# Eighteen of twenty-two block products of a gated MLP through Strassen's seven half products

## The chip, the core and the metric

The kernel runs on one core of a Trainium2 chip. The metric is the device time of one execution in microseconds; three runs of the kernel before took 979.35 to 979.56 us, with a median of 979.55.

## What is computed

One layer of a bidirectional encoder on 512 tokens of 1,024 features, in float32: a mixing part (short gated convolution and three groups of dilated window attention), a norm, and then the part that matters here, a gated MLP with a width-3 convolution over tokens and a last norm:

```
up = h @ w_up + b_up                       # 1024 -> 2 * 2816
a, gte = up[..., :D_FF], up[..., D_FF:]
f = gelu(dwconv3(a, ffn_conv_w) + ffn_conv_b) * gte
ffn = f @ w_down + b_down                  # 2816 -> 1024
h = layer_norm(ALPHA * h + ffn, ln2_g, ln2_b)
```

## The kernel before, in words

A float32 product runs as three matmuls on float32r parts: each operand is split into a high part (ScalarE, a cast by copy) and a low part (VectorE, the difference), and `mm3` (lines 363 to 366) issues high times high, high times low and low times high into one accumulator.

All weights lie in DRAM in the order of use, as chunks of up to 2,048 columns on 128 partitions (`chunk_plan`, line 65). `chunk(name, key)` (line 313) splits chunk i and i + 1 and issues the load of i + 2 from SyncE's queue; raw pieces of 1,024 columns have 3 buffers, high parts of 2,048 columns 3, low parts of 1,024 columns 5. The scheduler of the language orders each engine's instructions by program order and by when their inputs and buffers are ready, so splits can run further ahead than `chunk` asks.

The MLP has 22 blocks of 128 hidden features (lines 886 to 913). A hidden block takes two products of 24 matmuls on 512 tokens (`unit`, line 368); ScalarE adds the bias, GpSimd shifts rows for the convolution (`pad_shift`, line 669), ScalarE and VectorE convolve, ScalarE applies gelu, VectorE multiplies with the gate (line 907), and the result is split into a tile `f` of high and low part (lines 909, 910). From block 3 to 6 VectorE also scales one token group of the residual (`residual`, line 875).

The product with w_down goes token by token: the four tiles `hb` hold 128 tokens by 1,024 outputs. It comes in two parts, after block 10 and after block 21, each over the eleven blocks of its part and the two halves of 512 outputs. In the first part, and for the first half of the second, four accumulators run beside each other (lines 916 to 923) and VectorE adds each to `hb`. For the last half (lines 925 to 944) each token group takes its 33 matmuls in turn, and VectorE adds, takes statistics (`bn_stats`), finishes mean and deviation (`ln_finish`, line 333) and scales with two `scalar_tensor_tensor` a half; SyncE stores the result. The statistics of the first half are taken beside earlier work (line 931). The last group's half is cut into two times 256 columns, so that less work stands behind the last matmul.

The tiles of weights, activations and sums share one pool of 28 buffers of 1,024 columns (`blk`), the smaller ones another of 13 of 512 (`f32t`). Results of matmuls go through 8 accumulator banks in turn (`ps_any`).

Of the kernel before, what the change touches and what calls it, by code (L numbers as in the profile page):

```python
# [11 lines left out]
P = 128  # L12
# [5 lines left out]
FFH = NFF // 2  # L18
# [46 lines left out]
def chunk_plan():  # L65
# [13 lines left out]
    for part in range(2):  # L79
        for j in range(part * FFH, (part + 1) * FFH):  # L80
            out.append(("up", j, 2048))
        for half in range(2):
            for c, n in ((0, 4), (4, 4), (8, 3)):
                out.append(("dn", (part, half, c, n), n * 512))
    return out


def lay_out_weights(w):
# [10 lines left out]
    for name, key, cols in chunk_plan():  # L99
# [11 lines left out]
        elif name == "gate":  # L111
            c = [block(w_in, (BLK_GA + key) * P, P), block(w_in, (BLK_GB + key) * P, P)]
        elif name == "wo":
            half, kh = key
            c = [block(w_o[kh * 512 : (kh + 1) * 512], half * 512, 512)]
        elif name == "up":
            c = [block(w_up, key * P, P), block(w_up, DFF + key * P, P)]
        else:
            part, half, c0, n = key
            k0 = (part * FFH + c0) * P  # L120
            c = [block(w_down[k0 : k0 + n * P], half * 512, 512)]
# [53 lines left out]
def build(tc, x, wst, colt, dist, rows, vrow, out):  # L175
# [3 lines left out]
    with ExitStack() as ctx:  # L179
# [86 lines left out]
        offs = np.cumsum([0] + [P * c[2] for c in plan])  # L266
        splits = {}

        def load(i):
# [615 lines left out]
        g2 = b2 = None  # L885
        for part in range(2):
            ff = []
            for j in range(part * FFH, (part + 1) * FFH):
                w = chunk("up", j)
                if j < 2:  # L890
                    o = early[2 * j]
                    unit(o, w, 0, h1T, 256, 512)
                else:
                    o = ps_any()
                    unit(o, w, 0, h1T)
                u = small.tile([P, 768], F32, tag="upad", name=f"fp{j}", bufs=2)
                nc.scalar.activation(u[:, 128:640], o, AF.Identity, bias=col(C_BUP + j))  # L897
                pad_shift(u)
                a = conv3(u, C_FW + j, NFF)
                nc.scalar.activation(a, a, AF.Gelu, bias=col(C_FB + j))  # L900
                if j < 2:
                    o = early[2 * j + 1]
                    unit(o, w, 1024, h1T, 256, 512)
                else:
                    o = ps_any()
                    unit(o, w, 1024, h1T)
                nc.vector.scalar_tensor_tensor(a, o, col(C_BUP + NFF + j), a, op0=ALU.add, op1=ALU.mult)
                t = blk(F32R, (2, 512), f"f{j}")
                nc.scalar.activation(t[:, 0], a, AF.Copy)
                nc.vector.tensor_tensor(t[:, 1], a, f(t[:, 0]), op=ALU.subtract)  # L910
                ff.append(t)
                if 3 <= j < 7:
                    residual(j - 3)
            for half in range(2):
                ch = ((0, 4), (4, 4), (8, 3))
                if part == 0 or half == 0:
                    os_ = [ps_any() for _ in range(4)]
                    for c0, n in ch:
                        w = chunk("dn", (part, half, c0, n))
                        for r in range(4):  # L920
                            tok_mm(os_[r], ff, w, range(c0, c0 + n), r, c0, c0 == 0, c0 == 8)
                    for r in range(4):
                        add_to(hb[r], half, os_[r])
                else:
                    g2, b2 = row(6), row(7)
                    ws = [chunk("dn", (part, half, c0, n)) for c0, n in ch]
# [41 lines left out]
```

## Time and profile before

| | us |
|---|---|
| median of three runs | 979.55 |
| the profiled execution | 979.43 |
| its span | 977.6 |
| TensorE busy | 964.9 |
| VectorE busy | 552.9 |
| ScalarE busy | 395.9 |
| GpSimd busy | 55.8 |

The span runs from the first to the last event of the trace; the profiled execution has 1.83 us more around it. PE is TensorE's matmuls, PEld its weight loads, DVE VectorE, ACT ScalarE, POOL GpSimd, SP SyncE. Matmuls are pipelined, so the starts of two neighbours give the time of one better than the duration shown. Waits are put down to the instruction whose semaphore came last.

### The profile page before, as it was taken

How to read it: one execution, taken by the hardware profiler on the slowest of the kernel's cores; microseconds unless marked ns; L12 is line 12 of the kernel's file. 1: busy time of each engine (PE TensorE's matmuls, PEld its weight loads, DVE VectorE, ACT ScalarE, POOL GpSimd, SP SyncE). 2: the span in 40 equal slices, each digit the busy share in tenths (PEclk: the TensorE clock that was granted, in tenths of full speed). 3: DMA queues.
4: the chain of work that ended last, by engine and by line, in shares of the span. 5: the costliest groups of instructions: out<-in, count | busy, mean ns of one | idle time of the engine just before them, and what ended most of it. 6: DMA issues, size and time to landing. Idle time of an engine off the chain costs nothing.

```text
span 977.6 us, 11991 instructions
## 1 busy us (share of the span) xinstructions
PE 964.9 (99%) x4713; PEld 813.9 (83%) x4713; DVE 552.9 (57%) x886; ACT 395.9 (40%) x671; POOL 55.8 (6%) x163
## 2 busy tenths in 40 slices
PE   8999999999999999999999999999999999999996
PEld 7988888887888888888888888988888888888885
DVE  7856755968676444422445667659452255454266
ACT  4644465656543423223433323544441134444220
POOL 1000000000010001001000000011000001000000
PEclk9999999999999999999999999999999999999999
DMA  7313312221222123235324221352323243222412
GB/s 277 108 45 129 108 65 66 87 87 45 87 66 86 66 86 97 98 105 196 115 100 128 88 90 44 127 172 92 103 78 95 88 128 99 96 88 95 129 40 80
DMA packets 28217, 97.29 MB, mean 100 GB/s; under 512 B 3456, under 2 KB 3968, under 8 KB 28160
## 3 DMA queue, kind: packets, MB, share of 16 engines
q1 hardware_dynamic: 25776, 89.60, 28.0%
q0 software_dynamic: 2384, 6.92, 2.3%
q8 instruction: 37, 0.61, 0.3%
q14 instruction: 20, 0.16, 0.0%
HBM read 94.36 MB, written 2.15 MB: 99 GB/s over the span
## 4 chain that ended last, share of the span: by engine, by line
PE 96%; DVE 2%; DMA 1%; issue 0%; ACT 0%; DVEq 0%; POOL 0%; POOLq 0%
PE ps_acc L364 16%; PE ps_acc L366 16%; PE ps_acc L365 16%; PE ps_s L366 5%; PE ps_s L365 5%; PE ps_s L364 5%; PE ps_u L366 5%; PE ps_u L365 5%; PE ps_u L364 5%; PE ps_pt L365 4%; PE ps_pt L366 4%; PE ps_pt L364 4%; PE ps_pt L594 1%; PE ps_u L417 1%; PE ps_acc L417 1%
## 5 line engine op out<-in xcount | busy, mean ns | idle before, releaser
L307 DVE TENSOR_TENSOR lo<-raw,hi 128x1024 fp32r<-128x1024 f32 (+1 forms) x166 | 198.4, 1200 | 237.4 <-ACT hi L295 97.0
L295 ACT ACTIVATE hi<-raw 128x1024 fp32r<-128x1024 f32 x162 | 164.3, 1044 | 238.9 <-PE ps_acc L365 70.3
L364 PE MATMUL ps_acc<-hT,hi 128*128 128x512 f32 x416 | 164.2, 395 | 0.1
L366 PE MATMUL ps_acc<-hT,lo 128*128 128x512 f32 x416 | 162.3, 390 | 0.0
L365 PE MATMUL ps_acc<-hT,hi 128*128 128x512 f32 x416 | 162.0, 390 | 0.0
L366 PEld LDWEIGHTS ps_acc<-hT,lo 128*128 128x128 f32 x416 | 78.1, 188 | 16.7
L364 PEld LDWEIGHTS ps_acc<-hT,hi 128*128 128x128 f32 x416 | 78.2, 188 | 15.7 <-PE ps_acc L366 0.5
L365 PEld LDWEIGHTS ps_acc<-hT,hi 128*128 128x128 f32 x416 | 78.2, 188 | 15.5
L575 ACT ACTIVATE S<-S,nm 128x128 f32<-128x128 f32 (+2 forms) x96 | 40.1, 419 | 35.3 <-DVE nm L573 28.5
L365 PE MATMUL ps_acc<-h1T,hi 128*128 128x512 f32 (+1 forms) x96 | 36.0, 375 | 0.0
L364 PE MATMUL ps_acc<-h1T,hi 128*128 128x512 f32 (+1 forms) x96 | 35.8, 373 | 0.0
L364 PE MATMUL ps_pt<-h1T,hi 128*128 128x512 f32 (+1 forms) x96 | 35.6, 371 | 0.0
L365 PE MATMUL ps_pt<-h1T,hi 128*128 128x512 f32 (+1 forms) x96 | 35.6, 371 | 0.0
L366 PE MATMUL ps_pt<-h1T,lo 128*128 128x512 f32 (+1 forms) x96 | 35.6, 371 | 0.0
L364 PE MATMUL ps_u<-h1T,hi 128*128 128x512 f32 (+1 forms) x96 | 35.6, 371 | 0.0
L365 PE MATMUL ps_u<-h1T,hi 128*128 128x512 f32 (+1 forms) x96 | 35.6, 371 | 0.0
L366 PE MATMUL ps_u<-h1T,lo 128*128 128x512 f32 (+1 forms) x96 | 35.6, 371 | 0.0
L365 PE MATMUL ps_s<-h1T,hi 128*128 128x512 f32 (+1 forms) x96 | 35.6, 371 | 0.0
L364 PE MATMUL ps_s<-h1T,hi 128*128 128x512 f32 (+1 forms) x96 | 35.6, 371 | 0.0
L366 PE MATMUL ps_s<-h1T,lo 128*128 128x512 f32 (+1 forms) x96 | 35.6, 371 | 0.0
L366 PE MATMUL ps_acc<-h1T,lo 128*128 128x512 f32 (+1 forms) x96 | 35.6, 371 | 0.0
L673 POOL COPY fp<-fp 128x127 f32<-128x127 f32 x22 | 14.0, 636 | 317.9 <-ACT fp L897 317.9
(396 smaller groups left out, 2038.8 us busy)
## 6 DMA issues: line engine op xcount, KB each, us to landing
raw<-wst SPq DMA_DIRECT2D x160, 512.0 KB, 3.7
x<-x SPq DMA_DIRECT2D x4, 512.0 KB, 7.1
hb<-x POOLq DMA_DIRECT2D x4, 512.0 KB, 6.4
out<-hb SPq DMA_DIRECT2D x7, 256.0 KB, 2.1
ln_g<-rows POOLq DMA_DIRECT2D x3, 512.0 KB, 5.8
ln_b<-rows POOLq DMA_DIRECT2D x3, 512.0 KB, 7.0
raw<-wst SPq DMA_DIRECT2D x4, 256.0 KB, 2.6
vbias<-vrow POOLq DMA_DIRECT2D x1, 512.0 KB, 8.4
```

The source lines that it names most:

```text
L295: nc.scalar.activation(hi[:, part], Pieces(raws[i])[:, part], AF.Copy)
L307: ins = nc.vector.tensor_tensor(lo[:, part], Pieces(raws[i])[:, part], f(hi[:, part]), op=ALU.subtract)
L364: nc.tensor.matmul(o, ah, bh, start=start, stop=False)
L365: nc.tensor.matmul(o, ah, bl, start=False, stop=False)
L366: nc.tensor.matmul(o, al, bh, start=False, stop=stop)
L417: ins = nc.tensor.matmul(first[n][:, t], wk, hk, start=k == 0 and m == 0, stop=k == KT - 1 and m == 2)
L575: nc.scalar.activation(v, v, AF.Exp, bias=nm[:, j : j + 1], scale=0.125, accum_out=dn[:, j : j + 1])
L594: nc.tensor.transpose(pt[:, j * P : (j + 1) * P], self.pe[:, j * P : (j + 1) * P], ident)
L673: nc.gpsimd.tensor_copy(u[:, 1:128], u[:, 512:639])
```

## The change

Blocks 0 to 17 go in three parts of six blocks, that is three pairs of an even and an odd block. In a part the product is seen as one of 2 x 2 quarters: tokens 0 to 255 and 256 to 511, even and odd blocks, outputs 0 to 511 and 512 to 1,023. Strassen's scheme in Winograd's form makes it with seven products of half size (`STAGES`: Y, X1, W1, X2, V1, W2, V2), each 256 tokens by three blocks by 512 outputs.

The sums of activations (`pair_sums`) are made on VectorE once a pair is there, and split into high and low parts in place of the single blocks. The sums of weights U, T2, T3 and T4 (T2 with a fourth term) are made without an engine: a quarter is loaded plainly from SyncE's queue, and further quarters are added to it by transfers issued on GpSimd's queue that accumulate into the tile (`weight_sums`); signs are put on the activations. The steps are issued after hidden blocks 1 to 4 of a part, the fourth term after the first product. A sum has the columns of three blocks, 1,536, in pieces of 1,024 and 512, and is then split like a chunk; quarters used alone come as chunks.

The seven products of a part are issued after the first hidden block of the next one (`down`). Four of them go to accumulators in SBUF, kept over the three parts (ScalarE copies in the first part, VectorE adds in the others), three straight to `hb`; after the third part VectorE combines them with 16 additions of 512 columns. The last four blocks, 18 to 21, go token by token: for each of the four groups both halves of the outputs are made, added, and normalised; for the first group the matmuls of block 21 come last.

```
@@ -15,7 +15,9 @@
 KT = D // P
 NPAIR = 4
 NFF = 22
-FFH = NFF // 2
+
+NST = 6
+PARTS = 3
...
-    for part in range(2):
-        for j in range(part * FFH, (part + 1) * FFH):
-            out.append(("up", j, 2048))
-        for half in range(2):
-            for c, n in ((0, 4), (4, 4), (8, 3)):
-                out.append(("dn", (part, half, c, n), n * 512))
+    for j in range(NFF):
+        out.append(("up", j, 2048))
+        if j % NST == 0 and j > 0:
+            out += [("sd", (j // NST - 1, s[0]), 1536) for s in STAGES]
+    out += [("dn", half, 2048) for half in range(2)]
     return out
+STAGES = (
+    ("Y", None, "T2"),
+    ("X1", (0, 0), "R"),
+    ("W1", (0, 1), "U"),
+    ("X2", (1, 0), "R"),
+    ("V1", None, "T3"),
+    ("W2", (1, 1), "R"),
+    ("V2", None, "T4"),
+)
+QUARTER = {s[1]: s[0] for s in STAGES if s[1]}
...
+        def quarter(part, x, y):
+            i = where[("sd", (part, QUARTER[x, y]))]
+            return wst[int(offs[i]) : int(offs[i + 1])].rearrange("(p c) -> p c", p=P)
 
...
-        g2 = b2 = None
-        for part in range(2):
-            ff = []
-            for j in range(part * FFH, (part + 1) * FFH):
-                w = chunk("up", j)
...
-            for half in range(2):
-                ch = ((0, 4), (4, 4), (8, 3))
-                if part == 0 or half == 0:
-                    os_ = [ps_any() for _ in range(4)]
-                    for c0, n in ch:
-                        w = chunk("dn", (part, half, c0, n))
-                        for r in range(4):
-                            tok_mm(os_[r], ff, w, range(c0, c0 + n), r, c0, c0 == 0, c0 == 8)
-                    for r in range(4):
-                        add_to(hb[r], half, os_[r])
-                else:
-                    g2, b2 = row(6), row(7)
-                    ws = [chunk("dn", (part, half, c0, n)) for c0, n in ch]
-                    for r in range(4):
...
-                        for i, (a, b) in enumerate(zip(cuts, cuts[1:])):
-                            o = ps_any()[:, : b - a]
-                            for (c0, n), w in zip(ch, ws):
-                                tok_mm(o, ff, w, range(c0, c0 + n), r, c0, c0 == 0, c0 == 8, a - 512, b - 512)
-                            nc.vector.tensor_tensor(z[:, a:b], z[:, a:b], o, op=ALU.add)
-                            nc.vector.bn_stats(out=st[:, 1 + i, :], in_=z[:, a:b])
...
+        def hidden(j):
...
+        def high_low(t, a):
+            nc.scalar.activation(t[:, 0], a, AF.Copy)
+            nc.vector.tensor_tensor(t[:, 1], a, f(t[:, 0]), op=ALU.subtract)
+            return t
+        def pair_sums(i, a0, a1):
+            lo, hi = slice(0, 256), slice(256, 512)
+            k0 = tmp.tile([P, 512], F32R, tag="f32", name=f"k0{i}").rearrange("p (a b) -> p a b", a=2)
+            high_low(k0, a0[:, lo])
+            k1 = high_low(blk(F32R, (2, 512), f"k1{i}"), a1)
+            s13, s24 = f32t("s13"), f32t("s24")
+            nc.vector.tensor_tensor(s13[:, lo], a0[:, hi], a1[:, hi], op=ALU.subtract)
+            nc.vector.tensor_tensor(s13[:, hi], a0[:, lo], a0[:, hi], op=ALU.subtract)
+            nc.vector.tensor_tensor(s24[:, lo], s13[:, lo], a0[:, lo], op=ALU.subtract)
+            nc.vector.tensor_tensor(s24[:, hi], s24[:, lo], a1[:, lo], op=ALU.add)
+            s13 = high_low(blk(F32R, (2, 512), f"s13{i}"), s13)
+            s24 = high_low(blk(F32R, (2, 512), f"s24{i}"), s24)
+            return {"X1": (k0, 0), "X2": (k1, 0), "V2": (k1, 256), "W1": (s13, 0), "V1": (s13, 256), "Y": (s24, 0), "W2": (s24, 256)}
+        sums_of = {}
+        def weight_sums(part, step):
+            R = {q: quarter(part, *q) for q in QUARTER}
+            if step == 0:
+                main = {n: blk(F32, (1024,), f"w{n}") for n in ("U", "T2", "T3")}
+                tails = [blk(F32, (1024,), "wtail") for _ in range(2)]
+                tail = {"U": tails[0][:, :512], "T3": tails[0][:, 512:], "T2": tails[1][:, :512]}
+                for n in main:
+                    sums_of[n] = [main[n], tail[n]]
+                for n, st in (("U", "W1"), ("T2", "Y"), ("T2", "V2"), ("T3", "V1")):
+                    raws[where["sd", (part, st)]] = sums_of[n]
+                todo = [("T2", (0, 0)), ("U", (0, 0)), ("T3", (1, 1))]
+            else:
+                todo = {1: [("T2", (0, 1))], 2: [("U", (0, 1)), ("T3", (0, 1))], 3: [("T2", (1, 1))], 4: [("T2", (1, 0))]}[step]
+            for n, q in todo:
+                for t, src in zip(sums_of[n], (R[q][:, :1024], R[q][:, 1024:])):
+                    if step == 0:
+                        nc.sync.dma_start(out=t, in_=src)
+                    else:
+                        nc.gpsimd.dma_start(out=t, in_=src, accum_op=ALU.add)
+        acc = {}
+        def accumulators():
+            for n, st in enumerate(("X1", "V1")):
+                t = blk(F32, (2, 512), "acc" + st)
+                acc[st] = [t[:, s] for s in range(2)]
+            for st in ("Y", "W1"):
+                acc[st] = [f32t("acc" + st) for _ in range(2)]
+        def down(part, pairs):
+            if part == 0:
+                accumulators()
+            outs = {
+                "X2": [hb[s][:, :512] for s in range(2)],
+                "W2": [hb[s][:, 512:] for s in range(2)],
+                "V2": [hb[2 + s][:, :512] for s in range(2)],
+            }
+            for n, (st, _, _) in enumerate(STAGES):
+                w = chunk("sd", (part, st))
+                for s in range(2):
                     o = ps_any()
+                    for i, pr in enumerate(pairs):
+                        t, c0 = pr[st]
+                        a = slice(c0 + s * P, c0 + (s + 1) * P)
+                        b = slice(i * 512, (i + 1) * 512)
+                        mm3(o, t[:, 0, a], t[:, 1, a], w[0][:, b], w[1][:, b], i == 0, i == len(pairs) - 1)
+                    if st in acc and part == 0:
+                        nc.scalar.activation(acc[st][s], o, AF.Copy)
+                    else:
+                        d = (acc.get(st) or outs[st])[s]
+                        nc.vector.tensor_tensor(d, d, o, op=ALU.add)
+                if n == 0:
+                    weight_sums(part, 4)
+            if part == PARTS - 1:
+                for s in range(2):
+                    x1, y, w1, v1 = (acc[st][s] for st in ("X1", "Y", "W1", "V1"))
+                    (h00, h01), (h10, h11) = ((hb[r][:, :512], hb[r][:, 512:]) for r in (s, 2 + s))
+                    for d, t, op in (
+                        (h00, x1, ALU.add),
+                        (y, x1, ALU.add),
+                        (w1, y, ALU.subtract),
+                        (h01, w1, ALU.add),
+                        (h10, y, ALU.add),
+                        (h10, v1, ALU.add),
+                        (h11, w1, ALU.add),
+                        (h11, v1, ALU.subtract),
+                    ):
+                        nc.vector.tensor_tensor(d, d, t, op=op)
+        pairs, even, ff = [], None, {}
+        for j in range(NFF):
+            a = hidden(j)
+            if j >= PARTS * NST:
+                ff[j] = high_low(blk(F32R, (2, 512), f"f{j}"), a)
+            elif j % 2 == 0:
+                even = a
+            else:
+                pairs.append(pair_sums(j // 2 % (NST // 2), even, a))
+            part, q = divmod(j, NST)
+            if part < PARTS and 1 <= q <= 4:
+                weight_sums(part, q - 1)
+            if 3 <= j < 7:
+                residual(j - 3)
+            if q == 0 and j > 0:
+                down(part - 1, pairs)
+                pairs = []
+        g2, b2 = row(6), row(7)
+        ws = [chunk("dn", half) for half in range(2)]
+        k0 = PARTS * NST
+        for r in range(4):
+            z = hb[r]
+            cuts = (0, 512, 1024) if r < 3 else (0, 512, 768, 1024)
+            parts = list(zip(cuts, cuts[1:]))
+            st = small.tile([P, 3, 6], F32, tag="bnst2", name=f"l2{r}st", bufs=2)
+            o = [ps_any()[:, : b - a] for a, b in parts]
+            def part_sum(i, ks):
+                a, b = parts[i]
+                half = a // 512
+                tok_mm(o[i], ff, ws[half], ks, r, k0, ks[0] == k0, ks[-1] == NFF - 1, a % 512, a % 512 + b - a)
+            if r == 0:
+                for ks in (range(k0, NFF - 1), range(NFF - 1, NFF)):
+                    for i in range(2):
+                        part_sum(i, ks)
+            for i, (a, b) in enumerate(parts):
+                if r > 0:
+                    part_sum(i, range(k0, NFF))
+                nc.vector.tensor_tensor(z[:, a:b], z[:, a:b], o[i], op=ALU.add)
+                nc.vector.bn_stats(out=st[:, i, :], in_=z[:, a:b])
...
```

## Rows read from the trace of the kernel before

**Rows 1.** The page, part 1: busy time by engine.
```profile
span 977.6 us, 11991 instructions
...
PE 964.9 (99%) x4713; PEld 813.9 (83%) x4713; DVE 552.9 (57%) x886; ACT 395.9 (40%) x671; POOL 55.8 (6%) x163
```

**Rows 2.** The page, part 4: the chain that ended last, by engine.
```profile
PE 96%; DVE 2%; DMA 1%; issue 0%; ACT 0%; DVEq 0%; POOL 0%; POOLq 0%
```

**Rows 3.** Busy us of each engine by stretch: PE, PEld, DVE, ACT, POOL; clock, DMA share, GB/s.
```profile
730.00:790.00 60.00, 60.00 (x267) 49.69 (x266) 19.39 (x22) 11.67 (x14) 0.00 (x0) 1.00 0.30 92
790.00:909.00 119.00, 119.00 (x527) 98.57 (x526) 58.34 (x65) 50.41 (x66) 11.70 (x42) 1.00 0.32 102
```

**Rows 4.** PE in order of time, w_down product: start us, us, matmul.
```profile
734.83 0.39 PE L364 MATMUL ps_acc<-hi,f 128*128 128x512 f32 x1
...
745.71 0.39 PE L364 MATMUL ps_acc<-hi,f 128*128 128x512 f32 x1
...
961.26 0.28 PE L364 MATMUL ps_u<-hi,f 128*128 128x256 f32 x1
...
969.06 0.28 PE L366 MATMUL ps_acc<-hi,f 128*128 128x256 f32 x1
```

**Rows 5.** DVE in order of time, last norms: start us, us, operation.
```profile
953.99 0.69 DVE L936 TENSOR_TENSOR hb<-hb,ps_s 128x512 f32<-128x512 f32 x1 [1.43 <-PE ps_s L366]
...
957.20 0.69 DVE L931 BATCH_NORM_STATS2 l23st<-hb 128x6 f32<-128x512 f32 x1
...
958.36 1.41 DVE L943 SCALAR_TENSOR_TENSOR hb<-hb,l21mv,ln_b 128x512 f32<-128x512 f32 x2
...
961.47 0.69 DVE L936 TENSOR_TENSOR hb<-hb,ps_pt 128x512 f32<-128x512 f32 x1 [1.69 <-PE ps_pt L366]
962.19 0.69 DVE L937 BATCH_NORM_STATS2 l22st<-hb 128x6 f32<-128x512 f32 x1
...
966.71 0.41 DVE L936 TENSOR_TENSOR hb<-hb,ps_u 128x256 f32<-128x256 f32 x1
...
969.38 0.42 DVE L936 TENSOR_TENSOR hb<-hb,ps_acc 128x256 f32<-128x256 f32 x1 [1.79 <-PE ps_acc L366]
969.83 0.43 DVE L937 BATCH_NORM_STATS2 l23st<-hb 128x6 f32<-128x256 f32 x1
...
972.79 1.54 DVE L943 SCALAR_TENSOR_TENSOR hb<-hb,l23mv,ln_b 128x512 f32<-128x512 f32 x3
```

**Rows 6.** DVE groups from 600 us on: busy us, mean ns of one.
```profile
L307 DVE TENSOR_TENSOR lo<-raw,hi 128x1024 fp32r<-128x1024 f32 x63 | 77.0, 1224 | 75.8 <-PE ps_pt L366 22.5 <-PE ps_acc L366 19.3 <-PE ps_s L365 15.1
L910 DVE TENSOR_TENSOR f<-cv,f 128x512 fp32r<-128x512 f32 x22 | 15.2, 691 | 4.6 <-ACT f L909 4.6
L361 DVE TENSOR_TENSOR h1T<-lnT,h1T 128x256 fp32r<-128x256 f32 x16 | 6.3, 422 | 0.1
L307 DVE TENSOR_TENSOR lo<-raw,hi 128x512 fp32r<-128x512 f32 x4 | 2.8, 691 | 20.2 <-PE ps_s L365 13.6 <-PE ps_u L365 6.6
L836 DVE TENSOR_TENSOR hb<-hb,ps_u 128x512 f32<-128x512 f32 x4 | 2.7, 686 | 2.3 <-PE ps_u L366 2.3
```

**Rows 7.** ACT groups from 600 us on: busy us, mean ns of one.
```profile
L295 ACT ACTIVATE hi<-raw 128x1024 fp32r<-128x1024 f32 x62 | 62.8, 1054 | 93.1 <-PE ps_s L366 48.3 <-PE ps_u L366 24.1 <-PE ps_s L365 9.1
L897 ACT ACTIVATE fp<-ps_acc,cols 128x512 f32<-128x512 f32 x11 | 7.6, 690 | 30.0 <-PE ps_acc L366 30.0
```

**Rows 8.** Waits from 634 to 968 us: us in total, times, longest us.
```profile
ACT hi L295 <- PE ps_s L366: 48.3, 6, 9.2
...
SPq L277 <- DVE lo L307: 280.6, 57, 11.0
```

**Rows 9.** The page, part 6: DMA issues, KB each, median us to landing.
```profile
raw<-wst SPq DMA_DIRECT2D x160, 512.0 KB, 3.7
...
hb<-x POOLq DMA_DIRECT2D x4, 512.0 KB, 6.4
...
vbias<-vrow POOLq DMA_DIRECT2D x1, 512.0 KB, 8.4
```

More of the change, by code (lines that the diff above doesn't have):

```diff
@@ L117, in lay_out_weights @@
             c = [block(w_up, key * P, P), block(w_up, DFF + key * P, P)]
-        else:
-            part, half, c0, n = key
-            k0 = (part * FFH + c0) * P
-            c = [block(w_down[k0 : k0 + n * P], half * 512, 512)]
+        elif name == "sd":
+            q = dict((s[0], s[1]) for s in STAGES)[key[1]]
+            if q is None:
+                continue
+            k0 = key[0] * NST + q[0]
+            c = [block(w_down[k * P : (k + 1) * P], q[1] * 512, 512) for k in range(k0, k0 + NST, 2)]
+        else:
+            c = [block(w_down[PARTS * NST * P :], key * 512, 512)]
         c = np.concatenate(c, axis=1)
@@ L265, in build @@
         plan = chunk_plan()
-        offs = np.cumsum([0] + [P * c[2] for c in plan])
+        offs = np.cumsum([0] + [P * laid_out(c) for c in plan])
         splits = {}
@@ new lines, in hidden @@
+        def hidden(j):
+            w = chunk("up", j)
+            if j < 2:
+                o = early[2 * j]
+                unit(o, w, 0, h1T, 256, 512)
+            else:
+                o = ps_any()
+                unit(o, w, 0, h1T)
+            u = small.tile([P, 768], F32, tag="upad", name=f"fp{j}", bufs=2)
+            nc.scalar.activation(u[:, 128:640], o, AF.Identity, bias=col(C_BUP + j))
+            pad_shift(u)
+            a = conv3(u, C_FW + j, NFF)
+            nc.scalar.activation(a, a, AF.Gelu, bias=col(C_FB + j))
+            if j < 2:
+                o = early[2 * j + 1]
+                unit(o, w, 1024, h1T, 256, 512)
+            else:
+                o = ps_any()
+                unit(o, w, 1024, h1T)
+            nc.vector.scalar_tensor_tensor(a, o, col(C_BUP + NFF + j), a, op0=ALU.add, op1=ALU.mult)
+            return a
@@ new lines, in build @@
+        pairs, even, ff = [], None, {}
[5 more added lines that the diff above has]
+                even = a
+            else:
+                pairs.append(pair_sums(j // 2 % (NST // 2), even, a))
[7 more added lines that the diff above has]
+                pairs = []
@@ new lines, in build @@
+        g2, b2 = row(6), row(7)
[20 more added lines that the diff above has]
+                nc.vector.bn_stats(out=st[:, i, :], in_=z[:, a:b])
+            ((mean, rstd),) = ln_finish([st[:, : len(parts)]], f"l2{r}")
+            for a, b in parts:
+                s = slice(a, b)
+                nc.vector.scalar_tensor_tensor(z[:, s], z[:, s], mean, g2[:, s], op0=ALU.subtract, op1=ALU.mult)
+                nc.vector.scalar_tensor_tensor(z[:, s], z[:, s], rstd, b2[:, s], op0=ALU.mult, op1=ALU.add)
+                nc.sync.dma_start(out=outr[r][:, s], in_=z[:, s])
```

37 lines of the change are left out of this document (3 added, 34 removed).

## The prediction

> **What bounds the kernel now.** I read the page's shares first: TensorE (PE) is busy for 964.9 of 977.6 us [rows 1], and in the chain that ended last PE holds 96% [rows 2]. Since a share of busy time says little about single stages, I then read the stretches of the MLP: in the product of the first eleven blocks with w_down and in the eleven hidden blocks after it PE is busy for every microsecond at a granted clock of 1.00, the 2.4 GHz level, while VectorE (DVE) is busy for 19.4 of 60 and 58.3 of 119 us [rows 3]. The reader is to see two things: no wait of PE is left to remove, so time comes only from matmuls not issued; and DVE and ScalarE (ACT) have room, about half of it in the hidden blocks. Then the matmuls' order of time for their pace, the end of DVE's order of time for what follows the last matmul, the waits for how early the weight splits run, and the transfers.
>
> **The matmuls removed.** Six blocks took 6 x 4 token groups x 2 halves x 3 (high-high, high-low, low-high) = 144 matmuls of 512 columns. Strassen takes 7 products x 2 token groups x 3 block pairs x 3 = 126. Three parts make 54 fewer; nothing else on PE changes but the last output group's split into 256 columns, which falls from 33 pairs to 12. From 734.83 to 745.71, 48 matmuls of 512 columns start, so one is 0.2267 us [rows 4]; 54 are 12.24 us. From 961.26 to 969.06, 66 matmuls of 256 columns start, 0.12 us each [rows 4]; a pair costs 0.24 - 0.2267 = 0.0133 us more than a whole one, so 21 fewer pairs give 0.28 us. The last matmul, now at 969.06, would start at 969.06 - 12.52 = 956.54 if PE stays gapless. If all of it came through, the span would be 965.1 us.
>
> The Trainium skill's page "TensorE: Matmul & The Clock Gate" (section "Wait — 56ns, not 53.3ns?") gives 215.7 ns from start to start for 512 columns. The rows show 226.7 ns, so the measurement decides; by the page's figure the first term would be 11.6 us instead.
>
> **The end of the kernel.** Here I expect much of the gain to be given back. Before, the last half of the output took 33 matmuls a token group, 7.5 us on PE, and only that half's add and statistics came after them. Now both halves of a group come last: 24 matmuls, 5.44 us, and DVE must add both, take both statistics, and normalise. Group 2 of before took DVE from 961.47 to the next start at 966.71, 5.24 us, back to back, with one add and one statistics [rows 5]. A second pair costs 0.72 us each (961.47 to 962.19; the statistics' 0.69 and the same step), so 6.68 us a group against PE's 5.44: DVE sets the end. As a lower value, group 1 ran from 953.99 to 959.69 (the two last operations at 958.36, at the 1.33 us that group 2's two take), 5.70 us with a statistics of another group inside; without it 4.98, since independent work filled the gaps of the short dependent operations [rows 5]. So a group costs 6.42 to 6.68.
>
> Group 3 took 969.38 to 972.79 + 1.54 = 974.33, 4.95 us [rows 5]; its 512 columns add 1.44 and its first 256 add 0.41 + 0.43 and two steps of 0.03, 0.90: together 7.29. PE spends 84 x 0.2267 + 24 x 0.12 = 21.92 us on the final product, so with the last start at 956.54 it begins at 934.74. The first group runs blocks 18 to 20 for both halves (18 matmuls), then block 21 (3 and 3), so its first half is done after 21, 4.76 us; an add starts 0.21 us after the next matmul (961.47 after 961.26 [rows 4, 5]): DVE begins at 939.71. Then 3 x 6.42 to 3 x 6.68 + 7.29: it ends at 966.3 to 967.0, against 974.33 now. From there to the span's end the last store and closing stay: 977.6 - 974.33 = 3.27. Span 969.5 to 970.3, middle 969.9, so 7.7 us less. The profiled execution took 979.43, 0.12 below the median of the runs; 979.43 - 7.7 = **971.7 us**.
>
> **What I cost at nothing, and its cover.** *Stages of Strassen.* A stage lasts 18 x 0.2267 = 4.08 us on PE. DVE must split 1,536 columns (1.224 + 0.691) and make two adds (0.686 each): 3.29 us [rows 6]. ACT makes the high parts, 1.5 x 1.054 = 1.6, and in the first part for four stages two copies, nearest row 0.69 each [rows 7]: 3.0 us. Both fit, DVE with 0.8 us a stage over. Without that cover a stage would run at the slower engine's pace. The splits run early: in the whole MLP no split's wait ends with a transfer; the high parts wait for matmuls that free a buffer, and the loads wait for splits [rows 8]. With three buffers of high parts a split starts once the chunk two before it is done.
>
> *Pair sums.* A hidden block keeps DVE busy 58.34 / 11 = 5.3 us of 10.88 [rows 3]. A pair of blocks loses two subtractions of 0.691 and gains three of 0.691 and five operations on 256 columns of 0.422 [rows 6]: 2.8 us more a pair, 6.7 a block. ACT exchanges two casts for four. Blocks 3 to 6 carry the residual besides, as before.
>
> *The last combination*, 16 adds of 512 columns at 0.69 [rows 6], is 11.0 us of DVE after the third part. Those whose inputs are complete can use the 0.8 us of seven stages, 5.6; the rest, 5.4, lies beside block 19, where DVE has 10.88 - 5.3 = 5.6 free, with two more blocks before the final product. Without cover it adds up to 11.
>
> *Transfers.* A part is 6 x 10.88 + 28.6 = 93.9 us and moves 6.3 MB for w_up, 2.4 for the three plain quarters, 2.4 for the first loads of sums and 3.9 for five adding transfers (two pieces each): 15 MB, 159 GB/s, or 201 if an adding transfer counts twice. Before, 102 GB/s took 0.32 of the DMA engines [rows 3], so 0.5 to 0.63. No row shows an adding transfer. Its lower bound is a plain load of 512 KB from SP, 3.7 us; POOL's take 6.4 and 8.4 [rows 9]; the upper bound I take as twice the longest, 16.8 (read and write of the target). Nearest is POOL's plain load, as POOL issues both; I take some 10 us. Behind the waiting adds on POOL stand the shifts of the next hidden block, for which ACT's convolution waits; this delays splits that are about a block ahead. The tightest is the fourth term of T2: it waits for the split of Y and must land before V2's split, 6 x 4.08 - 3.5 = 21 us after Y begins. Even 16.8 fits. The first three terms are added one hidden block apart or more, 10.9 us. On SP, the six first loads of a part stand before w_up loads, while each of those has about a block of lead. So nothing at either end short of 21 us, and no gain.
>
> **The rivals.** *PE sets the end.* If short operations interleaved so well that DVE kept up with 5.44 us a group, the span would be 965.1 and the time 966.9. Against it: even with gaps filled a group costs 6.42. Chance 0.10.
>
> *Stages at DVE's pace.* If other DVE work (combination, next splits) falls in the stages and each of the 14 stages of parts two and three takes 0.45 us longer (4.08 to 4.5), 6.3 us are lost: 978. It decides once DVE has over 4.08 us a stage, one add of 512 columns and a bit more beyond the 3.29. For it: the margin is thin and DVE keeps order; against: split buffers lead by more than a stage. Chance 0.08. The removed matmuls are counted in the code, so "it does nothing" could only come out as such an offset.
>
> *Adding transfers come too late (the slower side).* Three terms on one buffer are serial, the next can only start when the one before has landed, and the fourth stands on the deadline above. With a landing of L us for a quarter, each part stalls PE by L - 21. The gain of 7.7 is gone at L = 23.6, and at L = 30 the time is 971.7 + 27 = 999. For it: no row prices such a transfer; against: it needs over three times POOL's plain load. Chance 0.12.
>
> The Trainium skill's "DMA: Bandwidth & Descriptors" ("Rules for kernel authors") asks that an accumulating DMA wait for the earlier DMA's semaphore on the same bytes. No run here shows this; it states the same serial chain and gives no duration.
>
> **How the numbers follow.** My own forecast, DVE at the end with all else hidden, has 0.70, range 969 to 974 (a few tenths for each of the three new hand-overs between hidden blocks and stages). With the rivals at 0.10, 0.08 and 0.12, the range that leaves out 2 in 10 goes from 966.8 (PE sets the end) to 977.5 (most of the second rival), and leaves out the late transfers. A measurement of this kernel tells a change of 0.2%, 2 us, from none: faster means below 977.6. Forecast and first rival make 0.80, with a little of the second, 0.81; the rest of the second, 0.06, is the same; slower 0.13.
>
> **What would show it.** Right: 54 fewer matmuls of 512 columns, PE gapless to about 956.5, then DVE back to back for 26 to 28 us to the end, and chain shares of DVE at about 3% instead of 2%. The first rival shows as DVE idle before each add of the last groups. The second shows PE gaps inside the stages that end with a split of VectorE; the third shows gaps of several us before V2 or Y that end with an adding transfer, and POOL waiting long on one. Wrong altogether would be a PE gap of over 5 us in a hidden block, or TensorE's clock below 1.00 in the stages.

## The result and the profile after

The kernel after takes **973.59 us** (median of 4 runs, 973.40 to 973.88) beside 979.52 for the kernel before on the same chip: ratio 0.994, interval 0.9927 to 0.9952. The forecast was 971.7 in 966.8 to 977.5. The profiled execution took 973.47 us, with a span of 971.7.

The page, part 1, of the kernel after:
```profile
span 971.7 us, 12114 instructions
...
PE 953.9 (98%) x4638; PEld 803.2 (83%) x4638; DVE 612.0 (63%) x1004; ACT 422.5 (43%) x719; POOL 83.5 (9%) x193
```
The page counts 75 matmuls fewer than [rows 1], as forecast: 54 removed, and 21 that are no longer cut in two. TensorE lost 11.0 us of busy time, of 12.5 forecast; the span lost only 5.9. The chain that ended last says where to look:
```profile
PE 89%; DVE 6%; DMA 2%; issue 1%; ACT 1%; POOL 0%; SPq 0%; DVEq 0%; POOLq 0%; ACTq 0%
```
PE held 96% of it before [rows 2]. DVE's 6% is more than the tail that was forecast, for which some 3% were put down; DMA's 2% (`ln_g<-rows`, by the page's lines) says that PE's row of matmuls is broken by something that began with a transfer. All waits of PE from 640 to 960 us:
```profile
PE ps_pt L393 <- ACT s L938: 2.2, 1, 2.2
PE ps_pt L395 <- DVE s L939: 0.3, 1, 0.3
```
There is one gap, in one place. PE around it, in order of time (start us, us, matmul, idle time before it and what ended it):
```profile
685.57 0.39 PE L393 MATMUL ps_pt<-hi,s 128*128 128x512 f32 x1
...
686.70 0.39 PE L395 MATMUL ps_pt<-hi,s 128*128 128x512 f32 x1
689.30 0.50 PE L393 MATMUL ps_pt<-hi,s 128*128 128x512 f32 x1 [2.21 <-ACT s L938]
...
690.37 0.80 PE L395 MATMUL ps_pt<-hi,s 128*128 128x512 f32 x1 [0.34 <-DVE s L939]
690.97 0.63 PE L393 MATMUL ps_u<-hi,s 128*128 128x512 f32 x1
691.39 0.63 PE L394 MATMUL ps_u<-lo,s 128*128 128x512 f32 x1
...
694.18 0.40 PE L393 MATMUL ps_acc<-hi,k 128*128 128x512 f32 x1
```
It is Y, the first Strassen product of part one. Two of its three pairs of blocks run; then PE waits for the high and low parts of the third pair's activation sum `s`. Y takes 694.18 - 685.57 = 8.61 us instead of 18 x 0.2267 = 4.08, so 4.53 us are lost. Only 2.55 of them are waiting. The rest is in the spacing of the starts after it, 0.43 us instead of 0.2267, and the stretches show why (busy us of PE, PEld, DVE, ACT, POOL; granted clock, DMA share, GB/s):
```profile
688.00:690.50 2.50, 0.86 (x3) 0.42 (x3) 2.32 (x4) 0.63 (x1) 2.50 (x2) 0.90 0.00 0
690.50:694.00 3.50, 3.50 (x10) 2.78 (x11) 2.02 (x3) 1.41 (x3) 0.34 (x3) 0.58 0.34 89
694.00:698.00 4.00, 4.00 (x19) 3.33 (x18) 3.13 (x4) 4.00 (x8) 0.00 (x0) 1.00 0.35 119
```
After the idle time the granted clock fell near its half level, 1.2 GHz, and was back at 694. A gap of PE costs more than it shows as waiting: here 4.53 for 2.55.

Why was the sum late? DVE was busy all through the gap, so it was behind. Its order of time, 25 us earlier:
```profile
660.42 1.22 DVE L336 TENSOR_TENSOR lo<-raw,hi 128x1024 fp32r<-128x1024 f32 x1
668.29 0.69 DVE L815 TENSOR_SCALAR ln_g<-ln_g 128x1024 f32<-128x1024 f32 x1 [6.65 <-DMA ln_g<-rows]
669.02 1.23 DVE L908 TENSOR_TENSOR hb<-hb,ln_g 128x1024 f32<-128x1024 f32 x1
...
686.10 1.21 DVE L909 TENSOR_TENSOR hb<-hb,ln_b 128x1024 f32<-128x1024 f32 x1
...
689.64 0.68 DVE L939 TENSOR_TENSOR s<-s,s 128x512 fp32r<-128x512 f32 x1
```
DVE stood still for 6.65 us for the row `ln_g` of the residual's scale. From 668.29 on it works without a break on what had piled up: the residual (lines 908 and 909), the convolution of two blocks, splits and pair sums. The low part that PE waits for comes last, at 689.64. And the row was late because of what GpSimd issued before it:
```profile
639.50 0.88 POOL L978 DMA_DIRECT2D wT<-wst  x1
...
649.30 1.71 POOL L978 DMA_DIRECT2D wT<-wst  x2 [4.14 <-DMA wT<-wst]
...
651.80 1.47 POOL L978 DMA_DIRECT2D wtail<-wst  x1
652.34 1.48 POOL L810 DMA_DIRECT2D ln_g<-rows  x1
```
The last of eight adding transfers (line 978) goes out at 651.80, the row at 652.34, and lands at 668.29, 15.9 us later. The DMA issues say the same (KB each, median us to landing):
```profile
wT<-wst POOLq DMA_DIRECT2D x12, 512.0 KB, 9.5
wtail<-wst POOLq DMA_DIRECT2D x15, 256.0 KB, 12.6
...
b_down<-rows POOLq DMA_DIRECT2D x1, 512.0 KB, 15.1
```
The other end of the chain is the tail. DVE's last norms: the first addition, one later addition with what follows it, and the second scalings of the token groups:
```profile
943.59 0.68 DVE L1072 TENSOR_TENSOR hb<-hb,ps_pt 128x512 f32<-128x512 f32 x1
...
948.63 0.68 DVE L1072 TENSOR_TENSOR hb<-hb,ps_acc 128x512 f32<-128x512 f32 x1
949.23 0.16 DVE L370 RECIPROCAL l20mv<-l20mv 128x1 f32<-128x1 f32 x1
...
952.50 1.41 DVE L1078 SCALAR_TENSOR_TENSOR hb<-hb,l20mv,ln_b 128x512 f32<-128x512 f32 x2
...
957.32 1.40 DVE L1078 SCALAR_TENSOR_TENSOR hb<-hb,l21mv,ln_b 128x512 f32<-128x512 f32 x2
...
962.27 1.41 DVE L1078 SCALAR_TENSOR_TENSOR hb<-hb,l22mv,ln_b 128x512 f32<-128x512 f32 x2
...
966.87 1.54 DVE L1078 SCALAR_TENSOR_TENSOR hb<-hb,l23mv,ln_b 128x512 f32<-128x512 f32 x3
```
From scaling to scaling it takes 4.82 and 4.95 us, but that is not the price of a group: the operations of neighbouring groups are mixed, and each of the two stretches holds one wide operation less than a group has. The price that can be set beside the forecast's 6.42 to 6.68 [rows 5] comes from the whole: DVE works for 24.82 us, and if the last group has its forecast 7.29 of them, the three others take 5.84 each. Against the forecast the span comes out like this: the final product begins at 938.99 instead of 934.74 (+4.25, the gap of 4.53); DVE begins 4.60 us after that instead of 4.97 (-0.37); it works until 968.41, 24.82 us, instead of 26.55 to 27.33 (-2.12 from their middle); 3.29 us follow, as before. Together +1.76: 971.7 for 969.9. Two errors of opposite sign, each larger than the miss, so the total does not confirm the sum.

### The profile page after: what moved, and what is told of

The parts are those of the page before. It is cut to its first block, busy times and chain, and to the rows that moved or that the text cites. A ratio compares the mean times of both kernels' runs of the same rounds, so it can differ in the third digit from the quotient of the medians.

```text
span 971.7 us, 12114 instructions
## 1 busy us (share of the span) xinstructions
PE 953.9 (98%) x4638; PEld 803.2 (83%) x4638; DVE 612.0 (63%) x1004; ACT 422.5 (43%) x719; POOL 83.5 (9%) x193
## 3 DMA queue, kind: packets, MB, share of 16 engines
q0 software_dynamic: 6704, 18.71, 8.8%
HBM read 110.87 MB, written 2.15 MB: 116 GB/s over the span
## 4 chain that ended last, share of the span: by engine, by line
PE 89%; DVE 6%; DMA 2%; issue 1%; ACT 1%; POOL 0%; SPq 0%; DVEq 0%; POOLq 0%; ACTq 0%
PE ps_acc L393 16%; PE ps_acc L394 16%; PE ps_acc L395 16%; PE ps_s L394 5%; PE ps_s L395 5%; PE ps_s L393 5%; PE ps_u L394 4%; PE ps_u L395 4%; PE ps_u L393 4%; PE ps_pt L395 4%; PE ps_pt L393 4%; PE ps_pt L394 4%; DMA ln_g<-rows 2%; PE ps_pt L623 1%; PE ps_u L446 1%
## 5 line engine op out<-in xcount | busy, mean ns | idle before, releaser
L336 DVE TENSOR_TENSOR lo<-raw,hi 128x1024 fp32r<-128x1024 f32 (+1 forms) x164 | 192.9, 1182 | 169.2 <-ACT hi L324 95.2
L324 ACT ACTIVATE hi<-raw 128x1024 fp32r<-128x1024 f32 (+1 forms) x160 | 160.7, 1031 | 188.4 <-PE ps_acc L394 70.3
L702 POOL COPY fp<-fp 128x127 f32<-128x127 f32 x22 | 18.0, 816 | 288.3 <-ACT fp L924 288.2
L394 PE MATMUL ps_acc<-h1T,hi 128*128 128x512 f32 (+1 forms) x104 | 39.1, 376 | 0.0
L393 PE MATMUL ps_acc<-h1T,hi 128*128 128x512 f32 (+1 forms) x104 | 38.9, 374 | 0.0
L394 PE MATMUL ps_s<-h1T,hi 128*128 128x512 f32 (+1 forms) x104 | 38.8, 373 | 0.0
L393 PE MATMUL ps_s<-h1T,hi 128*128 128x512 f32 (+1 forms) x104 | 38.8, 373 | 0.0
L395 PE MATMUL ps_s<-h1T,lo 128*128 128x512 f32 (+1 forms) x104 | 38.7, 373 | 0.0
L708 DVE SCALAR_TENSOR_TENSOR cv<-fp,cols,cv 128x512 f32<-128x512 f32 x22 | 16.5, 750 | 30.3 <-ACT cv L707 30.3
L927 ACT ACTIVATE cv<-cv,cols 128x512 f32<-128x512 f32 x22 | 15.9, 723 | 39.9 <-DVE cv L709 39.9
L393 PE MATMUL ps_pt<-h1T,hi 128*128 128x512 f32 (+1 forms) x88 | 32.5, 370 | 0.0
L394 PE MATMUL ps_pt<-h1T,hi 128*128 128x512 f32 (+1 forms) x88 | 32.5, 370 | 0.0
L393 PE MATMUL ps_u<-h1T,hi 128*128 128x512 f32 (+1 forms) x88 | 32.5, 370 | 0.0
## 6 DMA issues: line engine op xcount, KB each, us to landing
wtail<-wst POOLq DMA_DIRECT2D x15, 256.0 KB, 12.6
```

The source lines that it names most:

```text
L324: nc.scalar.activation(hi[:, part], Pieces(raws[i])[:, part], AF.Copy)
L336: ins = nc.vector.tensor_tensor(lo[:, part], Pieces(raws[i])[:, part], f(hi[:, part]), op=ALU.subtract)
L393: nc.tensor.matmul(o, ah, bh, start=start, stop=False)
L394: nc.tensor.matmul(o, ah, bl, start=False, stop=False)
L395: nc.tensor.matmul(o, al, bh, start=False, stop=stop)
L702: nc.gpsimd.tensor_copy(u[:, 1:128], u[:, 512:639])
```

## The experiments

Ten kernels. The first four change the kernel after, the others the first of them.

**Are the residual's rows the cause?** Their loads are moved ahead of all adding transfers; in the program the residual itself stays where it was, and takes its rows from `rows0` (those lines are left out here):
```
+            if j == 1:
+                rows0.extend([row(3), row(4), row(5)])
             a = hidden(j)
```


> The three rows that the residual of blocks 3 to 6 needs are loaded from GpSimd's queue before the first adding transfer instead of behind six of them. Theory A (the rows wait behind adding transfers: ln_g lands after 15.9 us, VectorE stands 6.6 us for it with the convolutions of blocks 4 and 5 behind, and the last pair sums of part one come 3.4 us late): the gap of TensorE at the first Y goes, and with it the stretch at the half clock; from the first matmul of Y to the first of X1 it takes 4.1 us instead of 8.6, so the time falls by 4.3 to 4.7 us, to about 969.1. Theory B (VectorE has too much work in blocks 3 to 6 whatever the rows do): most of the gap stays, Y takes 7 us or more, the time falls by less than 1.5 us.

969.83 us (969.54 to 969.95), ratio 0.9902 [0.9887, 0.9916]; 3.76 us faster than the kernel after. `ln_g` lands in 5.5 us, PE waits for nothing from 640 to 960, the final product begins at 935.06, and the chain has lost its DMA:
```profile
PE 92%; DVE 6%; ACT 1%; DMA 0%; issue 0%; DVEq 0%; ACTq 0%
```
So the gap goes away with the place of three loads of 512 KB, which stood behind the sums (eight adding transfers in the trace, where the expectation says six). But this run does not yet refute theory B, too much work for DVE in blocks 3 to 6. With its rows there, DVE took up the residual over 50 us earlier, before this stretch, so its work left the stretch too. Its first multiplication in each group (median ns, first and last start) in the kernel after, in this one, and in the third experiment, whose transfers do not add:
```profile
L908 DVE TENSOR_TENSOR hb<-hb,ln_g x4: 1208/1216/1225, 669.0 to 684.0; 128x1024 f32<-128x1024 f32 x4
L912 DVE TENSOR_TENSOR hb<-hb,ln_g x4: 1216/1220/1226, 612.9 to 632.5; 128x1024 f32<-128x1024 f32 x4
L908 DVE TENSOR_TENSOR hb<-hb,ln_g x4: 1215/1220/1227, 661.2 to 677.1; 128x1024 f32<-128x1024 f32 x4
```
The third experiment settles it: there the residual stays in the stretch, DVE is busy for 37.51 us from 634 to 680 where the kernel after has 29.75, and PE waits for nothing. Theory A holds.

**GpSimd's queue, or the DMA engines?** The rows stay where they are in the program, behind the sums of block 3, but are issued from SyncE's queue:
```
+            if j == 3:
+                for k in (3, 4, 5):
+                    t = blk(F32, (1024,), ROWS[k])
+                    nc.sync.dma_start(out=t, in_=rows[k : k + 1, :].partition_broadcast(P))
+                    rows0.append(t)
```


> The same three rows stay at their place behind the sums of part one, but are issued from SyncE's queue. If the rows were late because GpSimd's own queue was held up (issued late, or behind the adding transfers in that queue), ln_g lands within 4 to 8 us of its issue and the gap at the first Y goes: about 969 to 970. If the 16 DMA engines were simply full with adding transfers, the landing stays over 12 us wherever the rows are issued, and the time stays at 972 to 974.

974.69 us (973.0 to 975.37), 0.9946 [0.9929, 0.9963]. The gap stays (PE waits 4.2 us once), and the rows take as long from the other queue:
```profile
ln_g<-rows SPq DMA_DIRECT2D x1, 512.0 KB, 13.4
ln_b<-rows SPq DMA_DIRECT2D x1, 512.0 KB, 15.8
b_down<-rows SPq DMA_DIRECT2D x1, 512.0 KB, 18.2
```
That speaks against GpSimd's queue as the cause, and for what is under way in the DMA engines, but it is not a clean test. The scheduler issued the rows at 638.11, 14 us earlier than GpSimd had, right behind six first loads of the sums on the same queue and before the first adding transfer (639.97); `ln_g` was there at 651.5, well before the 668.3 of the kernel after. And the gap came about in another way than there. DVE's waits from 640 to 700 us:
```profile
DVE ln_g L908 <- DMA ln_g<-rows: 7.3, 1, 7.3
DVE k L943 <- ACT k L942: 5.1, 1, 5.1
```
The second is for ScalarE, whose casts stood behind a piece of weights that took 21.0 us to land: the rows moved the lateness from themselves to a weight load. Both experiments show that a load beside the sums is late; the next one tells why.

**Is it the adding, or the bytes?** The same transfers without the addition, so that the weight sums hold only the quarter loaded last (left out: the sums of weights):
```
-                        nc.gpsimd.dma_start(out=t, in_=src, accum_op=ALU.add)
+                        nc.gpsimd.dma_start(out=t, in_=src)
```


> The transfers on GpSimd's queue write instead of adding, so the weight sums hold only the last quarter loaded; number, size, order and queue stay. If adding is what makes them slow (read and write of the target), the median landing of a 512 KB piece falls from 9.5 to about 6 us, ln_g lands in under 10 us, and the gap at the first Y shrinks by half or more (time 970 to 972). If they are slow because many are in flight on one queue, the landings stay at 9 to 12 us, and so does the time, 973 to 974.

969.01 us (968.76 to 969.59), 0.9895 [0.988, 0.9909], and no wait of PE. Stretches of the kernel after (columns as above):
```profile
634.00:680.00 46.00, 46.00 (x205) 38.09 (x204) 29.75 (x40) 17.44 (x26) 12.63 (x25) 1.00 0.77 217
720.00:760.00 40.00, 40.00 (x178) 33.10 (x177) 21.80 (x32) 18.10 (x26) 9.68 (x20) 1.00 0.83 228
```
and of this one:
```profile
634.00:680.00 46.00, 46.00 (x205) 38.10 (x204) 37.51 (x50) 21.86 (x32) 12.02 (x31) 1.00 0.63 236
720.00:760.00 40.00, 40.00 (x178) 33.15 (x177) 25.20 (x36) 19.82 (x28) 8.69 (x22) 1.00 0.61 226
```
At the same rate the DMA share is 0.61 instead of 0.83 from 720 to 760. GpSimd's queue over the whole span (packets, MB, share of the 16 engines), in the kernel after and in this one:
```profile
q0 software_dynamic: 6704, 18.71, 8.8%
q0 software_dynamic: 5744, 18.71, 5.4%
```
With plain transfers `ln_g` lands in 8.6 us behind the same neighbours (landings from 634 to 680; `wT` took 10.6 there in the kernel after):
```profile
wT<-wst POOLq DMA_DIRECT2D x4, 512.0 KB, 6.9
...
ln_g<-rows POOLq DMA_DIRECT2D x1, 512.0 KB, 8.6
```
The addition makes the transfer slow, and the engines full for others: queue, order and sizes are the same.

**Is the tail DVE's?** Without the statistics of the second half of groups 0 to 2 (left out: half of the features in their mean and deviation):
```
+                if r == 3 or i == 0:
+                    nc.vector.bn_stats(out=st[:, i, :], in_=z[:, a:b])
```


> In token groups 0 to 2 the statistics of the second half of the outputs are left out, three operations of 0.69 us on VectorE (a step of 0.72 or less); the mean and deviation are those of the first half. If VectorE sets the end, its stretch from the first add to the last store shrinks by 3 x 0.6 to 3 x 0.72 and the time falls by 1.8 to 2.2 us, to about 971.6. If TensorE or the last group alone set the end, the time stays within 0.4 us of 973.6.

970.81 us (969.43 to 972.08), 0.9912 [0.9897, 0.9927]. The spread is probably the gap's, which is still there (3.0 us of waiting in the profiled execution of 972.08); the kernels without the gap spread by 0.3 to 0.8 us. DVE's tail is the cleaner reading, 944.32 to 966.99, 22.67 us for 24.82: 2.15 less. The end comes 5.47 us after the last matmul's start (961.52), in the kernel after 7.62 (960.79 to 968.41), and before 5.27 [rows 4, 5]. So some 2.3 us of the tail are DVE's delay and the rest is the last group's own chain.

**Can another engine take that work?** With the rows loaded early the last matmul starts at 956.85 (it ends at 957.1) and DVE ends at 964.47, again 7.62 us after that start. First, the second scaling of groups 0 to 2 on ScalarE and GpSimd:
```
-                nc.vector.scalar_tensor_tensor(z[:, s], z[:, s], rstd, b2[:, s], op0=ALU.mult, op1=ALU.add)
+                    nc.scalar.activation(z[:, s], z[:, s], AF.Copy, scale=rstd)
+                    nc.gpsimd.tensor_tensor(z[:, s], z[:, s], b2[:, s], op=ALU.add)
```


> The kernel with the residual's rows loaded early (969.8 us), and in the last norm, for token groups 0 to 2, the scaling with the deviation on ScalarE and the addition of the bias on GpSimd instead of one VectorE operation a half: VectorE loses six operations of 0.74 us, 4.4 us. With the rows early the last matmul starts at 957.1 and VectorE ends at 964.5; in the kernel before, an end followed the last matmul's start by 5.27 us, so 2.1 us of the end are VectorE's delay. Theory A, VectorE sets the end by that delay and not by its whole load: the time falls by those 2.1 us and no further, as PE then sets the end, to 967.7 (966.9 to 968.3). Theory B, as predicted, VectorE takes 6.4 us a group: it falls by 4.4 less what PE leaves, to 965.5. Theory C, ScalarE and GpSimd are slower than VectorE and their chain ends last, or they hold VectorE up: no gain or slower, 969.5 or above.

970.76 us (970.48 to 971.11), 0.9914 [0.99, 0.9927]: 0.9 slower. DVE beside GpSimd:
```profile
955.54 1.71 DVE L1084 SCALAR_TENSOR_TENSOR hb<-hb,l22mv,ln_g 128x512 f32<-128x512 f32 x1
...
961.74 1.41 DVE L1084 SCALAR_TENSOR_TENSOR hb<-hb,l23mv,ln_g 128x256 f32<-128x256 f32 x1
```
and GpSimd's operations:
```profile
953.70 3.00 POOL L1089 TENSOR_TENSOR hb<-hb,ln_b 128x512 f32<-128x512 f32 x2 [1.71 <-ACT hb L1088]
959.93 2.93 POOL L1089 TENSOR_TENSOR hb<-hb,ln_b 128x512 f32<-128x512 f32 x2 [3.23 <-ACT hb L1088]
```
An operation of 0.74 us takes 1.71 on DVE while GpSimd runs its 1.5 us ones, and one of 0.47 takes 1.41. Six DVE operations are stretched in this way, by 4.2 us together, as much as the 4.4 us taken away. Theory C holds, by its second branch: what is taken from DVE comes back as slower DVE. The Trainium skill's "SBUF — State Buffer" ("SBUF: two separate sides") has this: a DVE operation with two inputs in SBUF and a GpSimd operation that reads SBUF lock each other out for a whole instruction. The rows agree: all stretched operations read two inputs in SBUF, while an addition from an accumulator beside the same GpSimd work keeps its 0.67 us (950.68).

Second, the statistics of groups 0 to 2 on ScalarE, without GpSimd:
```
+                    nc.scalar.activation(junk, z[:, a:b], AF.Copy, scale=1.0 / D, accum_out=sq[:, i, 0:1])
+                    nc.scalar.activation(junk, z[:, a:b], AF.Square, scale=D**-0.5, accum_out=sq[:, i, 1:2])
```


> The kernel with the residual's rows loaded early (969.8 us), and in the last norm, for token groups 0 to 2, the statistics taken on ScalarE (two passes a half whose results are summed along the row: the mean, and the mean of the squares) instead of VectorE's six of 0.69 us; VectorE gains two more short operations a group. GpSimd does nothing. Theory A, VectorE's delay of 2.1 us behind PE at the end is all there is to win, since PE's last matmul stays at 957.1 and 5.27 us followed the last start before: 967.7 (967.2 to 968.4). Theory B, the predicted 6.4 us a group on VectorE without cover: 4.1 us less, 965.7. Theory C, ScalarE's two passes and the longer chain of a group end later than VectorE's statistics did: 969.5 or above.

969.74 us (969.53 to 969.96), 0.9902 [0.9886, 0.9919]: nothing, although DVE has 4.1 us of statistics less to do. Its idle time lies early (1.27, 1.13, 0.31 and 0.44 us before 948), and the short operations that end a group now stand bare, each waiting for the one before:
```profile
952.68 0.16 DVE L375 RECIPROCAL l21mv<-l21mv 128x1 f32<-128x1 f32 x1
952.87 0.16 DVE L376 TENSOR_TENSOR l21mv<-l21mv 128x1 f32<-128x1 f32 x1
...
953.64 1.41 DVE L1096 SCALAR_TENSOR_TENSOR hb<-hb,l21mv,ln_b 128x512 f32<-128x512 f32 x2
```
The statistics had filled these gaps. From the last matmul's start (957.18) to DVE's end (964.76) it is still 7.58 us. Theory A as written fell here: work taken from DVE doesn't shorten its delay wherever it is taken. The time is theory C's, and in the first group its reason shows too: ScalarE's passes, and a table load of 1.28 us that now stands right ahead of the square root (at 945.97, in the first experiment at 936.76), bring that group's reciprocal at 947.59, where it came at 945.29 with DVE's statistics. How much of the lost gain is that load alone, no run shows.

**Where in the line does work count?** The second scaling of one group left out (its outputs stay unscaled), once late, once early:
```
+                if r != 2:
                     nc.vector.scalar_tensor_tensor(z[:, s], z[:, s], rstd, b2[:, s], op0=ALU.mult, op1=ALU.add)
```


> The kernel with the residual's rows loaded early (969.8 us), with the second scaling (deviation and bias, two operations of 0.74 us, a step of 1.32 us together) of token group 2 in the last norm left out. Those two stand on VectorE between the last statistics and group 3's aggregation (at 958.34). Theory A, the end is set by what VectorE has in line after the last matmul: 1.3 us less, 968.5 (968.2 to 968.8). Theory B, the chain of short operations of group 3 sets it: within 0.3 us of 969.8.

> The same with the second scaling of token group 0 left out (at about 948.6), the same 1.32 us of VectorE but 14 us before the last matmul's end. Theory A1, VectorE is behind PE from the first group on, so that all its work counts: 1.3 us less, 968.5. Theory A2, only work late in the line counts, as earlier gaps are eaten by waits for sums and for the short operations: 969.4 to 969.9.

Group 2: 968.45 us (968.27 to 968.62), 0.9888 [0.9872, 0.9905], 1.38 less, as theory A has it. Group 0: 969.20 (968.93 to 969.64), 0.9897 [0.9882, 0.9912], 0.63 less, between its two theories. The same 1.32 us of DVE counts in full behind the last matmul, and about half 14 us earlier. The traces agree: DVE ends 6.31 us after the last matmul's start with group 2's left out, and 7.05 with group 0's, for 7.62.

**The last combination**, costed at nothing, left out (the Strassen terms kept in accumulators are then missing from the output):
```
-            if part == PARTS - 1:
+            if part == PARTS:
                 for s in range(2):
```


> The kernel with the residual's rows loaded early (969.8 us), with the last combination, 16 additions of 512 columns on VectorE (11.0 us), left out: the outputs of the first eighteen blocks then lack the Strassen terms kept in the accumulators. Predicted theory, the combination is hidden beside the last stages and block 19: the time stays, 969.3 to 970.2. Rival, it delays splits or the residue of work ahead of the final product: 0.5 us or more faster, up to 11.

969.72 us (969.58 to 969.97), 0.9903 [0.9889, 0.9916]: 11 us of DVE, and no time.

**The low parts ahead of the first addition.** The split of the last chunk is asked for before block 21:
```
+            if j == NFF - 1:
+                split(len(plan) - 1)
```


> The kernel with the residual's rows loaded early (969.8 us), with the split of the last weight chunk asked for before block 21, so that its two low parts on VectorE (2.35 us, right ahead of the first addition of the final product) come earlier. The first half's sum is complete 1.7 us before VectorE adds it, but VectorE then waits 0.5 us for the second half. Theory A, the second half is what VectorE waits for: VectorE starts up to 1.7 us earlier, has one addition and one statistics done sooner and stands idle longer; the time stays within 0.5 us of 969.8. Theory B, those two low parts hold up all of the end: 968.1 to 968.5. Or the order of the instructions does not move at all, and the time stays.

969.59 us (969.54 to 969.86), 0.9902 [0.9888, 0.9915]: no change beyond the runs' spread. The low parts did move, but the first addition came no sooner (940.63 beside 939.65, now waiting 2.16 us for PE, which took its matmuls in another order), so what it was to tell apart stays open. No version that computes the whole layer is faster than the first experiment's by more than the runs' spread.

## Why the prediction was right, and where it was wrong

**The matmuls removed: right.** With the rows early, the final product begins at 935.06 and the last matmul starts at 956.85, where 934.74 and 956.54 were forecast: 0.3 us for all new hand-overs, of "a few tenths for each".

**The transfers: the step that failed** is "nothing at either end short of 21 us, and no gain". Its parts were good. Adding transfers landed in 9.5 to 12.6 us by the medians of the tiles (forecast 10, bounds 3.7 to 16.8), the longest in 14.0; none kept its own product waiting; the rate from 695 to 880 is 163 GB/s at a share of 0.59 (forecast 159, 0.5 to 0.63):
```profile
695.00:880.00 185.00, 185.00 (x818) 153.19 (x817) 117.35 (x157) 88.05 (x121) 29.17 (x68) 1.00 0.59 163
```
Missing was who else loads in those microseconds. Only shifts and SyncE's loads were looked for behind the adds; "blocks 3 to 6 carry the residual besides, as before" took the residual as DVE work and not as three transfers with a due time. Before, they were issued at 649.54 and landed in 5.8 us; now at 652.34, behind eight adds, in 15.9. That became 4.5 us of PE, by a chain of four: transfer, DVE in order, activation sum, PE with the clock on top. The late-transfer rival (0.12) named the right resource, but its condition, a landing over 23.6 us, was never near. Of the marks of an error the second came true: a clock below 1.00 in a stage (0.58).

The Trainium skill's "DMA: Bandwidth & Descriptors" ("Rules for kernel authors") asks an accumulating DMA to wait for the earlier one on the same bytes; the trace agrees, with GpSimd's wait of 4.14 us for a `wT` transfer before it issues the next two.

**The end: the mechanism held in part, the size didn't.** DVE does set the end, as forecast: the chain leaves PE at 945.5 us and stays on DVE until 968.41. The mis-sized term is the group, 6.42 to 6.68 us forecast and some 5.84 in the trace (24.82 less 7.29, by three). The forecast added the second pair of operations at a step of 0.72 each, as for an operation whose follower waits for its result. In the kernel after the scheduler puts one group's operations between another's, and an addition then takes a step of 0.60 (948.63 to 949.23). Four such steps are some 0.5 us a group, an estimate that is most of the difference from 6.42. What the forecast also lacked is that DVE's load alone isn't the end. The rival "PE sets the end" is refuted, since work left out late in DVE's line shortens the time; but 4 us taken from DVE by way of another engine won nothing. In truth both count, 5.3 us of the last group's chain behind PE and 2.3 of DVE's delay.

**The sum came out by luck in part.** The gap cost 4.25 us that the sum had at nothing, and the tail gave 2.5 back. With the gap alone the time would have been 976.0, outside the 969 to 974 of the main forecast; with the tail alone it is 969.83, as measured without the gap, inside it.

**Stages at DVE's pace (0.08): refuted** in parts two and three, where PE has no wait. In the last of them DVE is nearly full, and PE doesn't feel it:
```profile
880.00:909.00 29.00, 29.00 (x129) 24.01 (x129) 28.29 (x42) 12.17 (x14) 0.00 (x0) 1.00 0.31 101
```
The split buffers' lead, put against this rival, covers it; leaving out the combination confirms that it costs nothing.

Open is why the waiting in the gap differs between profiled executions (2.55 us in the kernel after, 3.0 without half of the statistics), and how much of the last 2.3 us another order of DVE's line would save.

## What to carry to other kernels

When a change puts transfers on a busy stretch, list every other load that lands in that stretch with its due time, the small ones for a norm or a residual too, and move those with slack ahead; here three rows cost 3.8 us, and without that the change gives 9.5. An engine in order turns one late operand into a backlog that here reached TensorE 20 us later in another place, so follow a gap back past the engine that it names. At the end of a kernel, work counts by its place in the line: here what lay behind the last matmul counted in full and earlier work about by half, and moving it to another engine won nothing where that one slowed DVE, or lengthened a group's chain and left its short operations bare.

## What the runs showed of the hardware

A transfer that adds takes more of the DMA engines than a plain one of the same size: from 720 to 760 us the share per GB/s is 0.83 / 228 against 0.61 / 226, 1.35 times. For one transfer, GpSimd's queue gives an estimate: 18.71 MB took 8.8% of a span of 971.7 us with additions and 5.4% of 967.8 without, 85.5 and 52.3 us of all 16 engines. The 11.8 MB that add would take 33.0 us of the 52.3 plainly, so with addition they took 66.2, twice as long. Beside such transfers a 512 KB load took 13 to 18 us from either queue, and one 21.0, against 5.5 to 6.7 for the same three rows loaded early. GpSimd's additions of two tensors (1.5 us for 512 columns) stretched those VectorE operations beside them that read two tensors in SBUF, from 0.74 to between 1.00 and 1.71 us. And two waits of TensorE, 2.21 and 0.34 us with two matmuls between them, were followed by some 3 us at spacings of 0.43 us for 0.2267.
